# A pooling block, a gated recurrence and a 16,384-expert layer on one core: where 20 of the U tiles are transposed, and on which engine the low parts of one stage are made

## The chip, the cores and the metric

The kernel runs on one core of a Trainium2 chip. The metric is device time in microseconds (us): the median of three runs of the kernel before is 1994.73 us (1994.36 to 1997.6). A second time belongs to the one execution that was profiled, 1993.15 us, of which the profile's span covers 1991.4 us.

A core has five engines that run their own instruction streams in order: PE (matmul), DVE (vector), ACT (scalar), POOL (GpSimd) and SP, which here only issues DMA. They wait for each other through semaphores.

## The reference, cut to what matters

For 512 rows of 1024 columns, all in float32:

```
x = layer_norm(2**0.25 * x + pool_mixer(x), ln_g, ln_b)             # first block
ada = silu(c) @ w_ada + b_ada                                       # 6 shifts, scales, gates
z = modulate(rmsnorm(x)) @ w_in                                     # 5 sections of 512 columns
y_a = gate_b * causal_conv(gate_c * xa)
y_b = rg_lru(causal_conv(xr) + b) * gelu(gr)                        # a scan along the rows
x = x + g1 * (concat(head_rmsnorm(y_a), head_rmsnorm(y_b)) @ w_out)
h = modulate(rmsnorm(x))
q = h @ w_q; keys -> top 16 of 128, twice, 8 heads -> top 16 of 256 -> idx, g
x = x + g2 * sum_k g_k * gelu(U[idx_k] . h) * V[idx_k]              # U, V: 16384 x 1024
out = rmsnorm(x)
```

## The kernel before

Every large product is made from two halves of each float32 operand: a high part, rounded on ACT (`hi`), and a low part, the difference `src - hi` (`lo`). `mm3` (lines 139 to 141) then issues three matmuls: hi with hi, and two cross products. `split` makes both parts; its flag `pool` says whether the subtraction of the low part is on GpSimd (line 115) or on DVE (line 117). `wload` brings 512 KB of weights with one DMA (line 124) and splits them; it sends the low part to GpSimd when the count of loads is a multiple of `nload[1]`. That number is set stage by stage: 3 in the first block, `NZ` from the start of the product with `w_in`, none from the product with `w_q`, 2 from the dense expert part on. With `NZ = 1` all 31 weight tiles of `w_in` (20), `w_out` (8) and the first three heads of `w_q` have their low parts on GpSimd.

The stages, by the time in the profile:

- Up to about 353 us: the pooling block (line 339 to 343 also make the `ada` product on DVE beside it).
- 353 to 585 us, called the later front below: layer norm, `norm_T` (transposes of the rows by PE, line 461), the sections of `w_in` (`zchunk`, one chunk is 24 matmuls of 512 columns), two convolutions (lines 608 to 612), the recurrence `lru` (lines 635 to 660) and a head norm for each chunk (`headnorm`, lines 616 to 626, with a plain float32 matmul at line 620), then `w_out` (lines 737, 738) and the second norm.
- 585 to 955 us, called the middle: for 3 of the 4 row tiles the 16,384 experts are done densely. `q` and the key scores on PE, `top16` and `topk` on DVE (lines 856 to 860, 1012 to 1056), and from 743 us `g_tile`: DVE (1095, 1133) and ACT (1098, 1099) make one-hot tiles, PE multiplies them (1135), ACT copies the result out of PSUM (1136), and a DMA writes it to `g_d`. Beside this `stage_a` runs ahead: for tile `i` of 128 experts it computes gelu(U_i h) for 384 rows, 24 matmuls of 384 columns. `RT = 38` of the 128 tiles are done in the middle, 14 of them and 4 more ahead of `g_tile` in the program, the others spread through it by `run_a`.
- 955 to 1932 us, the main loop: for every tile of 128 experts `stage_v` multiplies gelu(U_i h) with the coefficients and V. The other 90 tiles of U are turned there by DVE. For the first row tile DVE and GpSimd gather rows of U and V instead (1181, 1193, 1204).

`stage_a` needs U_i with its columns on the partitions. In the middle there are two ways. Tiles `i < NU = 20` take way 4: `pre_u` has loaded them in the later front (160 DMAs of 64 KB, line 535, into `praw`), DVE has turned them in two halves each (`u_turn`, line 540, 40 instructions), and 40 DMAs have written them to the DRAM tensor `ut_d` (line 552); the middle loads them back (line 891) and splits them, ACT line 894 and DVE line 895, one instruction each of 1024 columns. The other 18 tiles take way 1 (`ATY`): the tile is loaded as it stands (line 878), PE transposes it in 8 pieces against an identity matrix into two of four PSUM side banks (line 882), and ACT (line 884) and DVE (line 886) make the high and low part from PSUM in two halves of 512 columns each.

`pre_u` is called once ahead of each of the 16 last chunks of `w_in` and turns one tile each time (`PU`), then the rest. The order on each engine is not the order of the code: a scheduler sets it from its own estimate of times, and the engines then keep to it. The lists under "The change" are of the built programs.

Of the kernel before, what the change touches and what calls it, by code (L numbers as in the profile page):

```python
# [33 lines left out]
AE = 5  # L34
T2 = ((0, 4), (4, 12))
AF_ = (1, 1, 0, 0)
NZ = 1
PRE = (('gn_b_2', 1), ('gn_b_2', 2))
TURN = {2: [('go', 1)], 3: [('lru', 0), ('conv', 0)], 6: [('lru', 1), ('go', 2)], 10: [('conv', 1), ('lru', 2), ('go', 3)], 
        13: [('lru', 3)], 14: [('conv', 2)]}  # L40
# [4 lines left out]
GP0 = 4  # L45
GL = 1
GE = 117
NU = 20
PU = (1,)
CB = 13  # L50
PL = 0
# [28 lines left out]
def _body(tc, nc, a, outer):  # L80
# [447 lines left out]
    U, W = a["expert_u_2"][0], a["expert_v_2"][0]  # L528
    ut_d = tc.dram_tile([max(1, NU), P, 2, KD * 64], F32, name="ut_d")
    npre = 0  # L530
# [11 lines left out]
    def pre_u(n):  # L542

        nonlocal npre
        for _ in range(n):
            if npre < NU:
                for h in range(2):
                    raw = up.tile([P, 2, 256], F32, name="praw", tag="praw")
                    u_load(raw, npre, 2 * h, 2)
                    ut = up.tile([P, KD, 64], F32, name="put", tag="put")  # L550
                    u_turn(ut, raw)
                    nc.sync.dma_start(ut_d[npre, :, h], ut.rearrange("p k e -> p (k e)"))
                npre += 1
# [35 lines left out]
    def zstart(sec, c):  # L589
        return wcols(a["w_in_2"][0], sec * 512 + c * P, P), bank()  # L590
# [83 lines left out]

    nload[1] = NZ
    zs = [zstart(*o) for o in ((3, 0), (4, 0), (3, 1), (4, 1))[:ZN]]
# [41 lines left out]

    pre_u(NU)

# [149 lines left out]
    def stage_a(i):  # L870
        uh = dn.tile([P, KD, P], F32R, name="uh", tag="uh", bufs=UB)
        ul = dn.tile([P, KD, P], F32R, name="ul", tag="ul", bufs=UB)
        ty = 4 if i < NU else ATY if i < RT else 2
        if ty != 1:
# [421 lines left out]
```

## Time and profile before

| | before |
|---|---|
| median of 3 runs | 1994.73 us |
| the profiled execution | 1993.15 us |
| its span | 1991.4 us |
| PE busy over the span | 1800.5 us (90%) |
| DVE busy | 1783.6 us (90%) |
| ACT busy | 830.8 us (42%) |
| POOL busy | 727.5 us (37%) |

PE and DVE are both busy for nine tenths of the span, so shares over the whole run say little about one stage. A stage is read from four views: the windows (what each engine does in a stretch, with the granted TensorE clock as a share of full speed), the groups of instructions (count, busy time, mean of one), the waits (who held whom), and the chain of waits, which is followed back from the last instruction of a stretch. Matmuls overlap each other: the step from one start to the next is what one costs, and the printed duration is longer.

### The profile page before, as it was taken

What the parts mean: (1) busy time and instruction counts of PE and PEld (TensorE: products, weight loads), DVE (VectorE), ACT (ScalarE), POOL (GpSimd) and SP (SyncE); (2) the same over time, 40 slices, a digit from 0 to 9 for tenths busy, and PEclk for the clock granted to TensorE, in tenths of its full rate; (3) what the DMA queues carried; (4) which work ended last, traced back from release to release, by engine and by line L of the source; (5) the groups of instructions that cost most, each with busy time, mean ns of one, the idle gap of its engine ahead of it and who ended that gap; (6) DMA issues with size and microseconds to landing.
All of it is one profiled execution on the core that took longest, in us unless ns stands there. A gap on an engine that the chain in (4) does not pass through costs nothing.

```text
span 1991.4 us, 26565 instructions
## 1 busy us (share of the span) xinstructions
PE 1800.5 (90%) x9003; PEld 1568.3 (79%) x9003; DVE 1783.6 (90%) x3088; ACT 830.8 (42%) x1318; POOL 727.5 (37%) x492
## 2 busy tenths in 40 slices
PE   8999889896899978888887999998999998989997
PEld 6787677765689978888766898888888887878886
DVE  8989888889868999996897998999999999999956
ACT  4433333444553339988332332333232333332334
POOL 3113222333351000000133655556565556565514
PEclk9999999998899989999998999999999999999999
DMA  5554574465554233545959999999999999999922
GB/s 163 180 166 128 190 250 131 140 203 179 172 159 135 76 112 139 202 179 205 294 199 281 299 285 292 302 296 309 306 298 296 310 299 289 305 293 306 293 102 96
DMA packets 288293, 441.13 MB, mean 222 GB/s; under 512 B 24600, under 2 KB 203652, under 8 KB 285084
## 3 DMA queue, kind: packets, MB, share of 16 engines
q1 hardware_dynamic: 251292, 305.19, 51.1%
q0 software_dynamic: 36864, 134.23, 20.5%
q8 instruction: 71, 1.16, 0.2%
q14 instruction: 66, 0.54, 0.1%
HBM read 393.11 MB, written 46.23 MB: 221 GB/s over the span
## 4 chain that ended last, share of the span: by engine, by line
DVE 36%; DMA 24%; PE 17%; issue 12%; ACT 7%; SPq 2%; POOL 2%; DVEq 0%; POOLq 0%; ACTq 0%
DMA uraw<-in_expert_u 11%; DVE ut L540 5%; DMA gu<-in_expert_u,idx 3%; DMA gv<-in_expert_v,idx 3%; DMA araw<-in_w_ada 3%; PE bank L139 3%; PE bank L141 3%; PE bank L140 3%; ACT gs L1136 2%; DVE acc L1204 2%; DVE ul L117 2%; DVE wlo L117 2%; ACT o L1098 2%; DVE junk L1193 2%; DVE sw L240 2%
## 5 line engine op out<-in xcount | busy, mean ns | idle before, releaser
L115 POOL TENSOR_TENSOR wlo<-wraw,whi 128x1024 fp32r<-128x1024 f32 x111 | 292.3, 2635 | 782.4 <-ACT whi L113 766.8
L141 PE MATMUL aux<-h2h,ul 128*128 128x384 f32 x1024 | 360.7, 353 | 59.8 <-DVE ul L117 53.5
L139 PE MATMUL aux<-h2h,uh 128*128 128x384 f32 x1024 | 355.9, 348 | 4.9 <-ACT uh L884 1.8
L140 PE MATMUL aux<-h2l,uh 128*128 128x384 f32 x1024 | 353.6, 345 | 0.0
L113 ACT ACTIVATE whi<-wraw 128x1024 fp32r<-128x1024 f32 x218 | 228.3, 1051 | 196.4 <-DMA wraw<-in_expert_v 68.5
L140 PE MATMUL o<-wlo,wh 128*128 128x512 f32 x756 | 297.7, 394 | 13.8 <-DVE wlo L117 13.7
L141 PE MATMUL o<-whi,wl 128*128 128x512 f32 x756 | 296.6, 392 | 0.0
L139 PE MATMUL o<-whi,wh 128*128 128x512 f32 x756 | 290.1, 395 | 5.2 <-ACT whi L113 5.2
L141 PEld LDWEIGHTS aux<-h2h,ul 128*128 128x128 f32 x1024 | 198.6, 194 | 76.6 <-DVE ul L117 68.7
L1181 POOL DMA_INDIRECT gv<-in_expert_v,idx x128 | 186.8, 1460 | 186.0 <-DVE acc L1204 150.4
L1181 POOL DMA_INDIRECT gu<-in_expert_u,idx x128 | 167.5, 1309 | 161.3 <-DVE junk L1193 127.7
L139 PEld LDWEIGHTS aux<-h2h,uh 128*128 128x128 f32 x1024 | 198.6, 194 | 10.3 <-ACT gl L905 2.4
L113 ACT ACTIVATE uh<-ut 128x1024 fp32r<-128x1024 f32 x90 | 95.3, 1058 | 262.2 <-PE aux L140 174.5
L540 DVE STREAM_TRANSPOSE ut<-uraw 128x1024 f32<-128x1024 f32 x90 | 200.0, 2222 | 4.7 <-DMA uraw<-in_expert_u 4.7
L140 PEld LDWEIGHTS aux<-h2l,uh 128*128 128x128 f32 x1024 | 197.9, 193 | 3.7
L1193 DVE SCALAR_TENSOR_TENSOR junk<-gu,hrow 128x1024 bf16<-128x1024 f32 x128 | 168.3, 1315 | 19.8 <-DMA gu<-in_expert_u,idx 19.6
L1204 DVE SCALAR_TENSOR_TENSOR acc<-gv,cf,acc 128x1024 f32<-128x1024 f32 x127 | 169.6, 1335 | 17.6 <-DMA gv<-in_expert_v,idx 15.1
L140 PEld LDWEIGHTS o<-wlo,wh 128*128 128x128 f32 x756 | 143.3, 190 | 43.9 <-DVE wlo L117 16.5
L113 ACT ACTIVATE wh<-gl 128x384 fp32r<-128x384 f32 x128 | 66.7, 523 | 253.2 <-PE o L140 234.3
L139 PEld LDWEIGHTS o<-whi,wh 128*128 128x128 f32 x756 | 143.3, 190 | 33.0 <-ACT whi L113 6.1
L141 PEld LDWEIGHTS o<-whi,wl 128*128 128x128 f32 x756 | 143.3, 189 | 30.7
L117 DVE TENSOR_TENSOR wlo<-wraw,whi 128x1024 fp32r<-128x1024 f32 x107 | 150.6, 1409 | 7.2 <-ACT whi L113 7.2
(376 smaller groups left out, 3607.4 us busy)
## 6 DMA issues: line engine op xcount, KB each, us to landing
wraw<-in_expert_v SPq DMA_DIRECT2D x128, 512.0 KB
uraw<-in_expert_u SPq DMA_DIRECT2D x360, 128.0 KB
araw<-in_w_ada SPq DMA_DIRECT2D x96, 256.0 KB
g_d<-gs SPq DMA_DIRECT2D x24, 1024.0 KB
gt<-g_d SPq DMA_DIRECT2D x15, 1536.0 KB
wraw<-in_pool_w_in SPq DMA_DIRECT2D x32, 512.0 KB
wraw<-in_w_in SPq DMA_DIRECT2D x20, 512.0 KB
praw<-in_expert_u SPq DMA_DIRECT2D x160, 64.0 KB
```

Source lines behind the costliest of these rows:

```text
L113: S.activation(hi, src, AF.Copy)
L115: G.tensor_tensor(lo, src, hi.bitcast(F32), op=OP.subtract)
L117: V.tensor_tensor(lo, src, hi.bitcast(F32), op=OP.subtract)
L139: i = PE.matmul(out, lhsT=l[0], rhs=r[0], start=first, stop=False)
L140: PE.matmul(out, lhsT=l[0], rhs=r[1], start=False, stop=False)
L141: PE.matmul(out, lhsT=l[1], rhs=r[0], start=False, stop=last)
L240: V.tensor_tensor(nxt[:, :, step:], cur[:, :, step:], cur[:, :, :T - step], op=OP.add)
L540: V.transpose(out=ut.rearrange("p k (a r) -> p a k r", r=32), in_=raw.rearrange("p a (c k) -> p a k c", k=KD))
L1098: S.activation(o2[:, u], iorow, AF.Abs, bias=sT[:, 1, t0 + u:t0 + u + 1], scale=-1.0)
L1181: G.indirect_dma_start(out=r, out_offset=None, in_=src, in_offset=bass.IndirectOffsetOnAxis(ap=idx[t][:, s:s + 1], axis=0))
L1193: paced(V.scalar_tensor_tensor(junk, r, 1.0, hrow[t], op0=OP.mult, op1=OP.mult, accum_out=cf[t][:, s:s + 1]))
L1204: paced(V.scalar_tensor_tensor(acc[t], r, cf[t][:, s:s + 1], acc[t], op0=OP.mult, op1=OP.add))
```

## The change

Two numbers change. With `NU = 0` nothing is turned ahead: `pre_u` does nothing, `ut_d` is not used, and `stage_a` takes way 1 for all 38 tiles. With `NZ = 1 << 30` no count is a multiple, so the 31 low parts of the later front are made by DVE.

```diff
 AF_ = (1, 1, 0, 0)
-NZ = 1
+NZ = 1 << 30
 PRE = (('gn_b_2', 1), ('gn_b_2', 2))
...
 GE = 117
-NU = 20
+NU = 0
 PU = (1,)
```

Instructions in the two built programs, by engine:

| engine | instruction | before | after |
|---|---|---|---|
| SP | DMA `praw<-in_expert_u` (L535) | 160 | 0 |
| SP | DMA `ut_d<-put` (L552) | 40 | 0 |
| SP | DMA `ut<-ut_d` (L891) | 20 | 0 |
| SP | DMA `uraw<-in_expert_u` (L878) | 18 | 38 |
| DVE | STREAM_TRANSPOSE `put<-praw` (L540) | 40 | 0 |
| DVE | `wlo<-wraw,whi` (L117) | 107 | 138 |
| POOL | `wlo<-wraw,whi` (L115) | 111 | 80 |
| PE | MATMUL `aux<-ident,uraw` (L882) | 144 | 304 |
| ACT | `uh<-ut` (L894), 1024 columns | 20 | 0 |
| ACT | `uh<-aux` (L884), 512 columns | 36 | 76 |
| DVE | `ul<-ut,uh` (L895), 1024 columns | 20 | 0 |
| DVE | `ul<-aux,uh` (L886), 512 columns | 36 | 76 |

DVE in the later front, inside the second `lru` (lines 654 to 660; `xr` is the next convolution). Before:

```order
L655 TENSOR_TENSOR s__3710<-s__3710,w__3711 128x512
L656 SCALAR_TENSOR_TENSOR r<-r,w__3711 128x512
L540 STREAM_TRANSPOSE put<-praw 128x2x8x32
L658 TENSOR_TENSOR s__3710<-s__3710,i 128x512
L540 STREAM_TRANSPOSE put<-praw 128x2x8x32
L659 SCALAR_TENSOR_TENSOR i<-r,s__3710 128x512
L660 TENSOR_TENSOR i<-i,ge 128x512
L610 TENSOR_SCALAR xr<-zr,cols 128x512
L612 SCALAR_TENSOR_TENSOR xr<-zr,cols,xr 128x511
L540 STREAM_TRANSPOSE put<-praw 128x2x8x32
L612 SCALAR_TENSOR_TENSOR xr<-zr,cols,xr 128x510
```

The same place on DVE after the change:

```order
L117 TENSOR_TENSOR wlo<-wraw,whi 128x1024
L655 TENSOR_TENSOR s__3662<-s__3662,w__3663 128x512
L656 SCALAR_TENSOR_TENSOR r<-r,w__3663 128x512
L658 TENSOR_TENSOR s__3662<-s__3662,i 128x512
L659 SCALAR_TENSOR_TENSOR i<-r,s__3662 128x512
L660 TENSOR_TENSOR i<-i,ge 128x512
L117 TENSOR_TENSOR wlo<-wraw,whi 128x1024
L610 TENSOR_SCALAR xr<-zr,cols 128x512
L612 SCALAR_TENSOR_TENSOR xr<-zr,cols,xr 128x511
```

The transposes are gone from between the steps of the recurrence, and low parts of weights stand there instead, fewer of them.

DVE in the middle, in the search for the top 16 of the first heads (`sc` are scores, `top` and `ti` values and places, `pos` and `pb` the places among the candidates). Before, one low part of a whole U tile:

```order
L1025 MAX_INDEX pos<-best,tmpk 128x8
L1051 TENSOR_TENSOR g<-best 128x48
L1033 CAST pb<-pos 128x48
L895 TENSOR_TENSOR ul<-ut,uh 128x2x8x64
L1042 TENSOR_TENSOR cmp__5617<-pb,offt 128x768
L1043 TENSOR_TENSOR prod<-cmp__5617,dt 128x768
L1044 TENSOR_REDUCE i_5335<-prod 128x48
L856 MAX top_5274<-sc 128x8 x2
```

The same place after the change:

```order
L886 TENSOR_TENSOR ul<-aux,uh 128x512
L1023 MAX best<-tmpk 128x8
L1025 MAX_INDEX pos<-best,tmpk 128x8
L1051 TENSOR_TENSOR g<-best 128x48
L1033 CAST pb<-pos 128x48
L1042 TENSOR_TENSOR cmp__5309<-pb,offt 128x768
L886 TENSOR_TENSOR ul<-aux,uh 128x512
L1043 TENSOR_TENSOR prod<-cmp__5309,dt 128x768
L856 MAX top_4954<-sc 128x8 x2
```

Halves of low parts, read from PSUM, stand where one whole low part stood. Ahead of the first top-16 instruction DVE has 5 whole low parts before and 5 halves after; ahead of its first `og` (L1133) it has all 20 whole ones before and 36 halves after.

PE in the middle, just ahead of the first matmul of `g_tile` (L1112 transposes the chosen indices and weights, L1135 is the product of one-hot tiles). Before:

```order
L1112 MATMUL aux<-ident,g 128x128
L139 MATMUL aux<-h2h,uh 128x384
L140 MATMUL aux<-h2l,uh 128x384
L141 MATMUL aux<-h2h,ul 128x384
L882 MATMUL aux<-ident,uraw 128x128 x8
L1135 MATMUL bank<-og,o_6753 128x128 x8
```

The place of the same three transposes of indices and weights (L1112) after the change:

```order
L1112 MATMUL aux<-ident,i_5015 128x128
L139 MATMUL aux<-h2h,uh 128x384
L140 MATMUL aux<-h2l,uh 128x384
L1112 MATMUL aux<-ident,i_5016 128x128
L1112 MATMUL aux<-ident,g 128x128
L882 MATMUL aux<-ident,uraw 128x128 x4
L141 MATMUL aux<-h2h,ul 128x384
```

Before, the first tile turned by PE stands right ahead of the first L1135, and 480 matmuls of 384 columns (20 tiles) stand in front of it. After, transposes stand between the matmuls from the first tile on: 160 of them (20 tiles) and 444 matmuls of 384 columns (18.5 tiles) are ahead of the first L1135. Ahead of the last matmul of key scores there are 233 matmuls of 384 columns before, and after the change 168 with 63 transposes.

## Rows read from the trace of the kernel before

**Rows 1.** Windows by stage: busy us (instructions) per engine; PEclk, DMA share.

```profile
353.00:402.00 49.00, 40.05 (x262) 36.46 (x261) 43.55 (x70) 23.68 (x51) 18.49 (x17) 0.93 0.48 146
402.00:540.00 138.00, 110.56 (x407) 80.72 (x406) 123.04 (x130) 69.60 (x90) 45.28 (x18) 0.89 0.61 191
585.00:720.00 135.00, 132.78 (x794) 126.13 (x794) 124.95 (x568) 53.88 (x84) 12.13 (x8) 1.00 0.43 136
720.00:757.00 37.00, 21.00 (x107) 20.46 (x106) 37.00 (x199) 19.50 (x42) 0.00 (x0) 0.72 0.10 38
757.00:955.00 198.00, 176.46 (x1283) 170.34 (x1282) 169.44 (x496) 182.16 (x341) 0.70 (x1) 1.00 0.53 195
```

**Rows 2.** Groups, 353 to 585 us: count, busy us, mean ns, idle before.

```profile
L540 DVE STREAM_TRANSPOSE put<-praw 128x512 f32<-128x512 f32 x40 | 46.2, 1158 | 12.8 <-DMA praw<-in_expert_u 12.7
L115 POOL TENSOR_TENSOR wlo<-wraw,whi 128x1024 fp32r<-128x1024 f32 x29 | 72.3, 2495 | 129.6 <-ACT whi L113 117.7 <-DMA praw<-in_expert_u 11.9
L612 DVE SCALAR_TENSOR_TENSOR cx<-gc,cols,cx 128x511 f32<-128x511 f32 x4 | 9.2, 2301 | 0.1
L612 DVE SCALAR_TENSOR_TENSOR xr<-zr,cols,xr 128x511 f32<-128x511 f32 x4 | 3.0, 746 | 0.1
```

**Rows 3.** Waits, 353 to 585 us: total, times, longest.

```profile
PE aux L620 <- ACT sq L616: 27.4, 5, 9.1
DVE put L540 <- DMA praw<-in_expert_u: 12.7, 6, 4.0
```

**Rows 4.** Chain of waits, 353 to 585 us: shares by line.

```profile
by line: DVE put L540 13.9%; issue 12.5%; DMA praw<-in_expert_u 10.1%; SPq L535 6.8%; PE bank L139 6.7%; PE bank L140 6.5%; PE bank L141 6.4%; DVE xr L612 2.9%; DVE cx L612 2.8%; DVE q L653 2.7%; DVE r L656 1.7%; SPq L552 1.6%; PE aux L620 
```

**Rows 5.** Timeline, GpSimd and then DVE, at 421 us: start, duration.

```profile
421.20 2.48 POOL L115 TENSOR_TENSOR wlo<-wraw,whi 128x1024 fp32r<-128x1024 f32 x1 [3.69 <-ACT whi L113]
421.36 2.88 DVE L656 SCALAR_TENSOR_TENSOR r<-r,w__3530 128x512 f32<-128x512 f32 x1
```

**Rows 6.** DVE, line 117, whole run: ns min/median/max; first, last start.

```profile
L117 DVE TENSOR_TENSOR wlo<-wraw,whi x107: 1202/1216/4129, 10.5 to 1956.4; 128x1024 fp32r<-128x1024 f32 x107
```

**Rows 7.** Groups on PE, 402 to 540 us: the plain fp32 matmuls.

```profile
L620 PE MATMUL aux<-sq,blk 128*128 128x512 f32 x13 | 11.7, 1010 | 27.4 <-ACT sq L616 27.4
L636 PE MATMUL aux<-xr,wri 128*128 128x512 f32 x8 | 4.1, 592 | 0.0
```

**Rows 8.** Timeline of PE at full clock: start, duration.

```profile
559.72 0.39 PE L140 MATMUL bank<-wlo,y 128*128 128x512 f32 x1
559.95 0.39 PE L141 MATMUL bank<-whi,y 128*128 128x512 f32 x1
...
574.92 1.05 PE L461 MATMUL aux<-ident,xn 128*128 128x128 f32 x8
...
649.36 0.34 PE L139 MATMUL aux<-h2h,uh 128*128 128x384 f32 x1
649.53 0.34 PE L140 MATMUL aux<-h2l,uh 128*128 128x384 f32 x1
```

**Rows 9.** Chain of waits again: one head norm on PE, start and us.

```profile
547.45 0.86 PE aux L620 x2
```

**Rows 10.** Groups, 585 to 757 us: low part of a tile turned ahead.

```profile
L895 DVE TENSOR_TENSOR ul<-ut,uh 128x1024 fp32r<-128x1024 f32 x20 | 24.3, 1214 | 3.2 <-ACT uh L894 3.2
```

**Rows 11.** Groups, 757 to 955 us: the pieces of a tile turned by PE.

```profile
L886 DVE TENSOR_TENSOR ul<-aux,uh 128x512 fp32r<-128x512 f32 x33 | 22.1, 681 | 17.6 <-ACT uh L884 17.6
L884 ACT ACTIVATE uh<-aux 128x512 fp32r<-128x512 f32 x33 | 19.8, 612 | 5.1 <-PE aux L882 5.1
L882 PE MATMUL aux<-ident,uraw 128*128 128x128 f32 x136 | 20.4, 276 | 2.9 <-ACT gl L905 2.9
```

**Rows 12.** Waits of PE, 585 to 757 us.

```profile
PE aux L1112 <- DVE i L1044: 9.2, 1, 9.2
PE bank L1135 <- ACT o L1099: 6.8, 1, 6.8
```

**Rows 13.** Chain of waits, 757 to 955 us: shares by line.

```profile
by line: ACT gs L1136 24.4%; ACT o L1098 20.8%; ACT o L1099 8.6%; issue 8.3%; PE bank L1135 7.5%; ACT uh L884 4.7%; DVE og L1133 3.4%; PE aux L141 3.1%; PE aux L139 3.1%; PE aux L140 2.8%; ACT gl L905 2.4%; DMA g_d<-gs 1.9%; DMA gt<-g_d 1.7
```

## Prediction

> **What bounds the kernel now.** I read the windows first, because PE and DVE are both at 90% over the whole run and only a stage shows which of them ends last. In the later front PE is the one that waits: in 402 to 540 us it is busy 110.6 of 138 us at a granted clock of 0.89, and DVE is busy 123.0 [rows 1]. At 585 to 720 us both are nearly full (PE 132.8, DVE 125.0 of 135), at 720 to 757 us DVE is full and PE idles 16 us, and at 757 to 955 us ACT is the fullest, 182 of 198 us [rows 1].
>
> Next the groups, the waits and the chain of the later front. The 40 transposes ahead of time take DVE 46.2 us there [rows 2]. PE's main wait is for the head norms, 27.4 us in 5 waits, and DVE itself waits 12.7 us for the pieces of U that it is to turn [rows 3]. The chain of waits says the same in another way: of its 232 us, 13.9% are these transposes, 10.1% the DMAs into `praw` and 6.8% their issue on SP, together 71 us [rows 4]. The work ahead of time is not hidden here; it is a large part of what ends last.
>
> A second cost is in the low parts on GpSimd. The same vector operation of 511 columns takes 2301 ns in one group of four and 746 ns in another [rows 2]. The timeline shows where the difference comes from: at 421.20 us GpSimd starts a low part of 2.48 us, and the DVE operation that starts at 421.36 lasts 2.88 us, about as long as the GpSimd one [rows 5]. So a low part on GpSimd can hold one DVE operation for about 2.1 us.
>
> **The change, part by part.**
>
> *Later front, DVE.* Busy in 353 to 540 us: 43.6 + 123.0 = 166.6 us [rows 1]. Taken away: 46.2 us of transposes [rows 2]. Taken away too: the holding by GpSimd. From below, the one group of four at 2301 ns gives 4 x 1.55 = 6 us; from above, each of the 29 low parts holds something for 2.1 us, 61 us. I take 25 us, somewhat under half, since only some low parts find DVE at such an operation. Added: 29 low parts at 1.216 us [rows 6], 35.3 us at most. DVE then has 166.6 - 46.2 - 25 + 35.3 = 130.7 us to do.
>
> *Later front, PE.* In 402 to 540 us it issues 407 matmuls [rows 1]. Of these 13 + 8 + 8 are plain float32 (line 635 has as many as 636) [rows 7], at 0.43 us each by the 0.86 us for two [rows 9], 12.5 us. The other 378 have 512 columns and step by 0.23 us at full clock [rows 8], 86.9 us. PE needs 99.4 us of the 138, so 38.6 us are waits and slow clock. In 353 to 402 us it is idle for another 9 us [rows 1]. At most 47.6 us can go; PE then needs 139 us in which DVE has 131. As DVE is still that full and works in a chain with ACT (recurrence, then head norm), the two won't fit without gaps. If PE's 27.4 us of waits for the head norms all stayed, 20 us would go; if all went, 48. I take 31, two thirds of the most, as about 71 us of the present chain vanish and at most 35 us come back.
>
> *Queues.* SP loses 160 + 40 issues in the later front, among which the weight loads stood; nothing is moved behind a longer wait there. In the middle 20 loads of `uraw` stand where 20 loads of `ut` stood.
>
> *Middle, ahead of the first L1135.* PE gets 152 more transposes and, by the built order, 36 fewer matmuls of 384 columns. Eight transposes took 1.05 us in the front [rows 8], 0.13 us each, so +19.9 us; the matmuls step by 0.17 us, so -6.1 us: +13.8 us on PE. From above, at the printed 276 ns each [rows 11], it is +42 - 6 = +36 us. Against this stand the 16 us that PE idles in 720 to 757 us, made up of its waits for the indices, 9.2 us, and for the one-hot tiles, 6.8 us [rows 12]; beside these it runs at a clock of 0.72 there [rows 1]. DVE ends this stretch, since it is the one that is full. Between its first top-16 instruction and its first `og` it has 31 halves at 681 ns [rows 11] in place of 15 whole low parts at 1214 ns [rows 10]: 21.1 - 18.2 = +2.9 us. But the first scores stand 36 matmuls earlier and 16 transposes later, -6.1 + 2.1 = -4.0 us. So DVE's end moves by -1 us if PE and ACT deliver in time, and by up to 36 - 16 = +20 if each transpose costs what is printed. I take +2, close to DVE's sum, as the gap in front of the indices is as wide as the work that PE gets.
>
> *Middle, from the first L1135.* The 36 matmuls and 8 transposes come back here: 6.1 + 1.0 = 7.1 us of PE; ACT gets 4 more halves at 612 ns, 2.4 us, DVE 4 at 681 ns, 2.7 us [rows 11]. The chain here is mostly ACT (lines 1136, 1098 and 1099 are 54%) with some PE [rows 13], so the price lies between 2.4 and 7.1; I take 5.
>
> At this place a rule of the Trainium skill speaks against the change. In 757 to 955 us 136 transposes by PE keep it busy for 20.4 us, 0.15 us each [rows 11], and the granted clock of that window is 1.00 [rows 1]. The page "TensorE: Matmul & The Clock Gate" (Part 4: PE-mode transpose) says that one took about 275 ns in a kernel and that transposes do not raise the clock as other matmuls do. By that figure the 160 transposes would be 44 us, an estimate from that page, and the sum 24 us worse, near no change; the trace has the same number as a printed duration but not as a step, so I keep 0.13.
>
> *Main loop.* Its instructions stay; its start on the DMA queues shifts. I take 0 (-4 to +4).
>
> **Sum.** -31 + 2 + 5 + 0 = -24 us on the profiled execution's 1993.15 us: 1969 us. The median of the runs is 1.6 us above that execution, so I forecast 1970 us. With the ends of the terms (-48 to -20; -1 to +20; +2.4 to +7.1; -4 to +4) the forecast's own range is 1955 to 1985.
>
> **Rivals.**
>
> *PE takes back all it lost.* With the transposes, the DMA waits and the holding gone, DVE has slack and PE runs through: -48 - 1 + 2 = -47, 1948 us. For it: DVE's 131 us are below PE's 139. Against: the chain between ACT and DVE inside each recurrence remains.
>
> *The middle takes it all.* The gap at 720 to 757 us is of no use, because each transposed tile needs ACT and then a DVE that is full before PE can go on, and each of the four side banks is held meanwhile. Then PE's +19.9 us all count, with 5 us after and about 5 us of waits: -31 + 30 = -1, 1994 us. For it: DVE is full there. Against: only the third product of a tile needs the low part, and the program puts the transposes of the next tile in front of it.
>
> *The low part's wait moves to DVE.* This one is slower. GpSimd now waits 117.7 us in front of its low parts for the high parts from ACT [rows 2], and nothing but the other low parts stands behind it. On DVE the same wait would hold the recurrence, the head norms and so PE. If a third of it, 39 us, meets a DVE that has other work, the front is 8 us slower, the middle 7 us: +15, 2010 us. It decides from 24 us on, a fifth of that wait. For it: DVE runs in order, and the loads that ACT waits for come through the same queue. Against: the scheduler puts the low part among other DVE work at the time when it expects the high part.
>
> *The clock falls in the middle.* If runs of transposes let it fall in 585 to 757 us as it does now in 402 to 540 us, to 0.89 [rows 1], 11% of 172 us is 19 us, of which PE's gap hides a few: 1985 us. It is the other half of the skill's rule; the 1.00 at 757 to 955 us speaks against it.
>
> *It doesn't do what it says.* The built program shows that all 38 tiles go through PE and 31 low parts move, so I give this nothing.
>
> **Chances and range.** Forecast 0.56, PE takes back all 0.12, the middle takes it all 0.10, the wait on DVE 0.17, the clock 0.05. No change means within 0.2%, 4 us, about what a measurement of this kernel can tell. Forecast, first rival, clock and a fifth of the second count as faster: 0.56 + 0.12 + 0.05 + 0.02 = 0.75; the third rival and 0.01 of the second are slower, 0.18; 0.07 of the second is the same. The range of 8 in 10 goes from 1945, just beyond the first rival, to 2000, which leaves out most of the third.
>
> **What would show it.** Right: the group of 511 columns at 2301 ns falls to about 750; PE's waits for the head norms fall below 12 us; the clock of the later front rises above 0.95; `w_out` and the second norm end near 554 us in place of 585; the middle lasts within 10 us of today's 370; PE's wait for the indices shrinks below 5 us. Wrong: new waits of DVE for ACT's high parts of more than 20 us in the later front; a middle over 385 us; a granted clock below 0.95 in 585 to 720 us; or a main loop that differs by more than 5 us from 1036 us, which nothing in this sum foresees.

## The result, and the profile after

The changed kernel takes 1963.42 us in the median of 4 runs (1957.91 to 1967.59); its ratio to the kernel before is 0.984, 95% interval 0.981 to 0.987. A second series of it gave 1955.43 us, ratio 0.981 (0.978 to 0.983). It is faster, by 31 us in the first series and, by the ratio, 39 in the second, where 24 were forecast. Its profiled executions took 1957.91 and 1951.71 us, against 1993.15 us and, for a second profile of the kernel before, 1997.54 us.

To compare stages that begin at different times I cut each trace at the same events: the first layer norm of the rows (line 501), the weight load of the first gate matmul (635), the first product that takes up a `w_out` result (737), the first copy of key scores (844), the first `og` (1133), the first and the last product `gl*gt` of the main loop (932). Lengths in us:

| from, to | before | before, again | after | after, again |
|---|---|---|---|---|
| start, layer norm | 336.2 | 337.3 | 338.9 | 337.3 |
| layer norm, gates | 65.9 | 67.4 | 64.9 | 64.8 |
| gates, `w_out` | 156.5 | 157.1 | 119.5 | 119.6 |
| `w_out`, scores | 60.4 | 60.4 | 57.8 | 61.2 |
| scores, first `og` | 126.1 | 127.0 | 128.0 | 128.0 |
| first `og`, main loop | 209.5 | 210.2 | 218.3 | 219.5 |
| main loop | 977.1 | 976.6 | 968.7 | 959.5 |
| rest | 59.7 | 59.8 | 60.0 | 60.0 |

"The front" below is the second and third row together: 222.3 us before, 184.4 after. The windows of the kernel before at these marks, as in [rows 1]. The columns are the stretch, its length, the busy us (instructions) of PE, of PE's weight loads, of DVE, ACT and GpSimd, then the granted clock, the DMA share and GB/s:

```profile
336.20:402.10 65.90, 54.55 (x345) 48.69 (x344) 59.93 (x100) 30.08 (x64) 25.82 (x25) 0.95 0.41 124
402.10:558.60 156.50, 129.06 (x487) 95.55 (x486) 134.81 (x144) 78.09 (x102) 52.90 (x21) 0.90 0.58 182
619.00:745.10 126.10, 113.23 (x621) 106.24 (x620) 125.76 (x694) 41.30 (x67) 0.00 (x0) 0.96 0.27 91
745.10:954.60 209.50, 182.67 (x1311) 176.56 (x1312) 180.95 (x536) 193.92 (x367) 0.30 (x1) 0.98 0.50 186
```

The same four of the changed kernel, and its main loop:

```profile
338.90:403.80 64.90, 53.32 (x347) 48.26 (x346) 53.50 (x103) 31.38 (x66) 5.96 (x17) 0.92 0.27 76
403.80:523.30 119.50, 119.50 (x490) 91.87 (x488) 93.67 (x130) 76.35 (x100) 0.00 (x0) 1.00 0.31 92
581.10:709.10 128.00, 123.80 (x725) 116.83 (x724) 127.16 (x710) 43.45 (x80) 0.00 (x0) 0.99 0.29 93
709.10:927.40 218.30, 195.21 (x1389) 191.19 (x1387) 183.47 (x541) 198.29 (x377) 0.87 (x1) 0.96 0.52 186
927.40:1896.10 968.70, 897.10 (x4278) 794.71 (x4277) 911.84 (x1122) 308.09 (x431) 509.04 (x316) 0.97 0.96 288
```

From the gates to `w_out` PE is now busy for every one of the 119.5 us, at a granted clock of 1.00 instead of 0.90; DVE is busy for 93.7 us where it was for 134.8. Of the 37.0 us that went, 27.4 are PE's waits for the head norms; the other 9.6 are busy time (129.1 against 119.5 us for about as many matmuls, 487 and 490 in the traces), at the lower granted clock. The groups of the front answer [rows 2 and 6]:

```profile
L117 DVE TENSOR_TENSOR wlo<-wraw,whi 128x1024 fp32r<-128x1024 f32 x30 | 36.6, 1220 | 15.5 <-ACT whi L113 15.5
L612 DVE SCALAR_TENSOR_TENSOR xr<-zr,cols,xr 128x511 f32<-128x511 f32 x4 | 3.0, 750 | 0.1
L612 DVE SCALAR_TENSOR_TENSOR cx<-gc,cols,cx 128x511 f32<-128x511 f32 x4 | 3.0, 744 | 0.0
```

The operation that took 2301 ns takes 744, and the low parts cost DVE 36.6 us and 15.5 us of waiting for ACT. All of PE's waits of the front, against [rows 3]:

```profile
PE aux L461 <- DVE rq L438: 8.0, 1, 8.0
PE aux L461 <- DVE xn L448: 2.9, 1, 2.9
PE bank L139 <- ACT ah L113: 0.6, 1, 0.6
```

The wait for the head norms (27.4 us) is gone. The chain of the front, against [rows 4], is now PE's three products, 63%, in place of transposes and their DMAs:

```profile
by line: PE bank L139 21.1%; PE bank L140 20.9%; PE bank L141 20.9%; DVE wlo L117 3.9%; issue 3.6%; PE aux L620 3.3%; DMA wraw<-in_w_in 2.3%; DMA wraw<-in_w_q 2.2%; PE aux L636 1.9%; PE aux L635 1.9%; DVE st L498 1.7%; ACT nf L469 1.6%; DVE
```

The instruction of [rows 5] that lasted 2.88 us beside GpSimd, in the timeline after (start, duration):

```profile
416.92 0.69 DVE L656 SCALAR_TENSOR_TENSOR r<-r,w__3530 128x512 f32<-128x512 f32 x1
```

In the middle, all of PE's waits from `w_out` to the first `og` [rows 12]:

```profile
PE aux L141 <- DVE ul L886: 3.7, 4, 2.0
PE aux L139 <- ACT uh L884: 0.8, 1, 0.8
PE bank L139 <- DVE ot L737: 0.6, 1, 0.6
PE aux L882 <- ACT gl L905: 0.5, 2, 0.3
```

The wait for the indices, 9.2 us, has vanished: the transposes fill it. From the first `og` to the main loop the groups of [rows 11] are:

```profile
L886 DVE TENSOR_TENSOR ul<-aux,uh 128x512 fp32r<-128x512 f32 x38 | 25.8, 685 | 12.2 <-ACT uh L884 12.2
L882 PE MATMUL aux<-ident,uraw 128*128 128x128 f32 x156 | 24.9, 282 | 11.2 <-ACT gl L905 11.2
L884 ACT ACTIVATE uh<-aux 128x512 fp32r<-128x512 f32 x39 | 23.1, 612 | 4.9 <-PE aux L882 3.4 <-DVE o L1095 1.5
```

PE's transposes now wait 11.2 us for ACT's gelu (line 905), 2.9 before, but all of PE's idle time in this stretch fell, from 26.8 to 23.1 us. Its busy time rose by 12.5 us: counted in the traces, it has 458 matmuls of 384 columns there in place of 401, and 154 transposes in place of 136.

### The profile page after: what moved, and what is told of

Same layout as the page of the kernel before. It is cut to its first block, busy times and chain, and to the rows that moved or that the text cites. A ratio compares the mean times of both kernels' runs of the same rounds, so it can differ in the third digit from the quotient of the medians.

```text
span 1956.1 us, 26521 instructions
## 1 busy us (share of the span) xinstructions
PE 1809.1 (92%) x9163; PEld 1587.4 (81%) x9163; DVE 1741.4 (89%) x3099; ACT 833.3 (43%) x1338; POOL 643.8 (33%) x461
## 4 chain that ended last, share of the span: by engine, by line
DVE 33%; PE 27%; DMA 24%; issue 8%; ACT 5%; POOL 2%; SPq 1%; DVEq 0%; POOLq 0%; ACTq 0%
DMA uraw<-in_expert_u 13%; DVE ut L540 4%; PE bank L141 4%; PE bank L140 4%; PE bank L139 4%; DMA gv<-in_expert_v,idx 3%; DMA gu<-in_expert_u,idx 3%; DVE wlo L117 2%; PE aux L141 2%; PE bank L1135 2%; PE aux L139 2%; PE aux L140 2%; DVE acc L1204 2%; DVE junk L1193 2%; DMA araw<-in_w_ada 2%
## 5 line engine op out<-in xcount | busy, mean ns | idle before, releaser
L115 POOL TENSOR_TENSOR wlo<-wraw,whi 128x1024 fp32r<-128x1024 f32 x80 | 210.9, 2637 | 642.7 <-ACT whi L113 640.8
L141 PEld LDWEIGHTS aux<-h2h,ul 128*128 128x128 f32 x1024 | 199.4, 195 | 79.5 <-DVE ul L117 66.5
L1181 POOL DMA_INDIRECT gv<-in_expert_v,idx x128 | 194.3, 1518 | 181.1 <-DVE acc L1204 153.4
L1181 POOL DMA_INDIRECT gu<-in_expert_u,idx x128 | 158.9, 1242 | 171.9 <-DVE junk L1193 119.2
L117 DVE TENSOR_TENSOR wlo<-wraw,whi 128x1024 fp32r<-128x1024 f32 x138 | 177.2, 1285 | 28.1 <-ACT whi L113 28.1
L540 DVE STREAM_TRANSPOSE ut<-uraw 128x1024 f32<-128x1024 f32 x90 | 199.5, 2218 | 2.4 <-DMA uraw<-in_expert_u 2.4
L1204 DVE SCALAR_TENSOR_TENSOR acc<-gv,cf,acc 128x1024 f32<-128x1024 f32 x127 | 174.5, 1374 | 17.4 <-DMA gv<-in_expert_v,idx 17.2
L1193 DVE SCALAR_TENSOR_TENSOR junk<-gu,hrow 128x1024 bf16<-128x1024 f32 x128 | 179.6, 1403 | 11.7 <-DMA gu<-in_expert_u,idx 11.4
## 6 DMA issues: line engine op xcount, KB each, us to landing
uraw<-in_expert_u SPq DMA_DIRECT2D x360, 128.0 KB
```

The lines of the kernel that those rows point to most:

```text
L115: G.tensor_tensor(lo, src, hi.bitcast(F32), op=OP.subtract)
L117: V.tensor_tensor(lo, src, hi.bitcast(F32), op=OP.subtract)
L141: PE.matmul(out, lhsT=l[1], rhs=r[0], start=False, stop=last)
L540: V.transpose(out=ut.rearrange("p k (a r) -> p a k r", r=32), in_=raw.rearrange("p a (c k) -> p a k c", k=KD))
L1181: G.indirect_dma_start(out=r, out_offset=None, in_=src, in_offset=bass.IndirectOffsetOnAxis(ap=idx[t][:, s:s + 1], axis=0))
L1193: paced(V.scalar_tensor_tensor(junk, r, 1.0, hrow[t], op0=OP.mult, op1=OP.mult, accum_out=cf[t][:, s:s + 1]))
```

## The experiments

Each kernel was timed in five rounds beside the kernel before; "ratio" is to it, with the 95% interval. First, which half of the edit made the front shorter. Theory A: DVE's transposes and their traffic held PE. Theory B: GpSimd's low parts did, by holding DVE's operations.

**The first edit alone**, on the kernel before:

```diff
-NU = 20
+NU = 0
```

> The kernel before with the first edit alone (`NU = 0`): nothing is turned ahead, the 31 low parts of the later front stay on GpSimd. The stretch meant is that from the first gate product (line 635) to the first `w_out` product (line 737), 156.5 us before and 119.5 after. Theory A (PE was held by the transposes ahead of time: DVE's own 46 us for them and the loads and stores that go with them): the stretch falls to 118-126 us and the time comes to 1960-1970 us, as after. Theory B (PE was held by GpSimd's low parts, which stretch DVE's operations by some 41 us in all): DVE keeps its long operations, the stretch only falls to 135-145 us and the time to 1975-1985 us.

Measured: 1969.32 us, ratio 0.987 (0.984 to 0.990). The two windows of the front (layer norm, then gates to `w_out`):

```profile
335.50:400.40 64.90, 53.54 (x335) 47.96 (x334) 53.95 (x90) 31.22 (x65) 26.29 (x25) 0.92 0.23 65
400.40:540.00 139.60, 123.42 (x486) 92.12 (x485) 108.40 (x113) 76.10 (x101) 52.92 (x21) 0.96 0.27 81
```

The stretch, 139.6 us, is B's, the time A's. It gets there by a main loop of 954.9 us, 22 us shorter than before, which neither theory spoke of (below); the stretches from `w_out` to the loop, 413.7 against 396.0 us, take 18 of these back. In the front the first edit alone is worth 18 of 38 us.

**The second edit alone:**

```diff
-NZ = 1
+NZ = 1 << 30
```

> The kernel before with the second edit alone (low parts of the later front on DVE): the 20 tiles are still turned ahead by DVE. Theory A: DVE has 46 us of transposes and 35 us of low parts in the later front, about 145 us of work in a stretch in which PE needs 119, so the stretch from line 635 to line 737 stays at 145-158 us and the time at 1985-2000 us. Theory B: no operation of DVE is stretched any more, the stretch falls to 125-135 us and the time to 1965-1975 us. In both the middle keeps its 370 us, so a front as short as that of the changed kernel would give about 1953-1957 us.

Measured: 1992.56 us, ratio 0.999 (0.996 to 1.001), no difference. The front:

```profile
337.40:411.10 73.70, 56.75 (x352) 50.98 (x351) 60.10 (x109) 30.79 (x65) 5.76 (x17) 0.86 0.45 131
411.10:560.50 149.40, 127.32 (x486) 95.14 (x484) 127.94 (x164) 77.86 (x101) 0.00 (x0) 0.91 0.59 183
```

The stretch is A's; with the layer norm 8 us longer, the front stays at 223.1 us. Alone, then, the two edits bring 18 and -1 us of front, together 38.

**GpSimd makes low parts a second time** in the later front of the changed kernel. The edit reaches the 20 weight tiles of `w_in`, not the 29 that the expectation speaks of:

```diff
+        if twice:
+            G.tensor_tensor(twice[0].tile([P, 1024], F32R, name="lo2", tag="lo2", bufs=1), raw, hi.bitcast(F32), op=OP.subtract)
```

> The changed kernel, in whose later front GpSimd makes each low part a second time into a tile that nothing reads; DVE's work and order stay as they are. Theory B (a GpSimd operation on two inputs holds an operation of DVE for about its own length): some 29 operations of 2.5 us on GpSimd, DVE's busy time in the stretch from line 635 to line 737 rises from 94 to 115-135 us, and the stretch from 119.5 to 130-145 us; the time comes to 1972-1988 us. Theory A (the holding matters little): DVE rises by less than 10 us, the stretch stays at 119-122 us, the time at 1958-1968 us.

Measured: 1987.55 us, ratio 0.997 (0.994 to 0.9995). The front:

```profile
334.80:411.20 76.40, 59.09 (x346) 52.83 (x344) 61.42 (x99) 30.78 (x65) 33.01 (x26) 0.84 0.21 59
411.20:554.30 143.10, 126.91 (x490) 95.42 (x490) 119.96 (x134) 77.51 (x101) 32.58 (x11) 0.93 0.27 79
```

As B expects, DVE's busy time rises from 93.7 to 120.0 us, and the stretch to 143.1. One form in it, held in one place and free in another (the lines of this kernel stand 3 lower in the file; its 658 is 655 elsewhere):

```profile
L658 DVE TENSOR_TENSOR s__3537<-s__3537,w__3538 128x512 f32<-128x512 f32 x1 | 2.8, 2849 | 0.0
...
L658 DVE TENSOR_TENSOR s__3887<-s__3887,w__3888 128x512 f32<-128x512 f32 x1 | 0.7, 695 | 0.0
```

The first ran beside a second low part on GpSimd, the second beside nothing there. The layer norm, 11.5 us longer, counts less: some of GpSimd's own steps of it now stand behind the second low parts.

**The transposes alone:** the changed kernel with 40 transposes by DVE of one resident tile:

```diff
+    still = up.tile([P, 2, 256], F32, name="still", tag="still", bufs=1)
+    u_load(still, 0, 0, 2)
...
-                    u_turn(ut, raw)
-                    nc.sync.dma_start(ut_d[npre, :, h], ut.rearrange("p k e -> p (k e)"))
+                    u_turn(ut, still)
```

> The changed kernel with 40 more transposes on DVE in the later front, all of one tile that is loaded once; nothing reads what they make, and the loads and stores of U stay away. Theory A1 (what the turning cost was DVE's own time): DVE's 94 us in the stretch from line 635 to line 737 become about 125, and as that stretch has so far lasted DVE's busy time and 21 to 31 us more, it grows from 119.5 to 140-152 us; the time comes to 1980-1995 us. Theory A2 (what it cost were the 200 DMAs and their issue on SP, 71 us of the chain of waits before together with the transposes): the stretch stays at 120-126 us and the time at 1955-1970 us.

Measured: 1985.44 us, ratio 0.995 (0.992 to 0.998). The front:

```profile
337.30:424.60 87.30, 63.25 (x374) 56.22 (x372) 83.29 (x134) 32.06 (x66) 6.04 (x17) 0.86 0.21 61
424.60:553.40 128.80, 118.39 (x462) 88.81 (x462) 104.77 (x140) 76.96 (x100) 0.00 (x0) 0.96 0.28 84
```

A1 has the time, and the front (216.1 us) is longer by what it expects, but not in the place that it names: the stretch, 128.8 us, is in neither theory's band. With no loads to wait for, the scheduler wrote many transposes early; in the chain twelve stand in a row (start, us):

```profile
397.62 11.69 DVE put L540 x12
```

**The traffic alone:** the changed kernel with the 160 loads of U and 40 stores, and no transposes:

```diff
-                    ut = up.tile([P, KD, 64], F32, name="put", tag="put")
-                    u_turn(ut, raw)
-                    nc.sync.dma_start(ut_d[npre, :, h], ut.rearrange("p k e -> p (k e)"))
+                    nc.sync.dma_start(ut_d[npre, :, h], raw.rearrange("p a d -> p (a d)"))
```

> The changed kernel with the 160 loads of U and the 40 stores to DRAM of before in the later front, the stores straight from the loaded tiles; no transposes, and nothing reads the stores. Theory A1: the stretch from line 635 to line 737 stays at 119-124 us, the time at 1955-1968 us. Theory A2: weights arrive later behind these DMAs and their issue, the stretch grows to 130-150 us, and the time comes to 1970-1990 us.

Measured: 1978.86 us, ratio 0.992 (0.989 to 0.995). From the gates to `w_out`:

```profile
404.30:556.20 151.90, 127.92 (x490) 95.26 (x488) 98.19 (x134) 78.37 (x102) 0.00 (x0) 0.91 0.65 195
```

The stretch is 2 us beyond A2's band and the time is A2's, with DVE hardly busier than after. The waits of the whole front, 340 to 556 us, name the reason, DVE's and then ACT's (us, times, longest):

```profile
DVE wlo L117 <- ACT whi L113: 46.8, 15, 8.8
```

```profile
ACT whi L113 <- DMA wraw<-in_w_in: 29.9, 8, 10.7
ACT whi L113 <- DMA wraw<-in_w_out: 15.8, 3, 11.7
```

The weights land late, ACT's high parts are late, and DVE, in order, stands in front of the low parts. This is the prediction's third rival, the wait that moves to DVE, at 46.8 us; it did not come with the change, which takes the traffic away at the same time, nor with the second edit alone (11.9 us in its front), where DVE is itself late. SP, which issues all these DMAs in order, stands in front of the loads and stores of U itself (the store, line 552 elsewhere, is line 550 in this kernel):

```profile
SPq L535 <- DMA ut_d<-praw: 31.7, 38, 2.8
SPq L550 <- DMA praw<-in_expert_u: 16.2, 33, 1.7
```

In the front of the kernel before, it stood in front of the stores for DVE's transposes:

```profile
SPq L552 <- DVE put L540: 42.9, 30, 4.6
```

So this kernel holds the queue in another way than the kernel before does, and its 31 us are not exactly the traffic's share there. No run took the bytes and the held queue apart; the DMA share of the stretch, 0.65 against 0.96 in the main loop, speaks for the queue.

**The middle spared:** the changed kernel with the middle of the kernel before (untransposed tiles are loaded, as the expectation says):

```diff
-NU = 0
+NU = 20
...
-            if npre < NU:
+            if npre < 0:
...
-            nc.sync.dma_start(ut.rearrange("p k e -> p (k e)"), ut_d[i].rearrange("p h d -> p (h d)"))
+            nc.sync.dma_start(ut.rearrange("p k e -> p (k e)"), U[i * P:(i + 1) * P, :])
```

> The changed kernel, whose first 20 U tiles are loaded in the middle with the load and the split of the kernel before, but without having been transposed (the result is that of untransposed tiles): the later front is that of the changed kernel, the middle that of the kernel before. From `w_out` to the main loop the changed kernel took 404 to 409 us, the kernel before 396. If the transposes on PE are the price of the middle, this kernel has 393-398 us there and ends 6-12 us below the changed kernel, at 1945-1956 us. If the middle is longer for another reason (an earlier start, another state of the DMA queues), it keeps 403-410 us and 1955-1966 us.

Measured: 1948.04 us, ratio 0.975 (0.971 to 0.979), and 392.1 us from `w_out` to the main loop, just below the band of the first guess: 12 to 17 us less than the changed kernel, 4 to 6 less than the kernel before. That the turning by PE costs this much is not shown, though. From `w_out` to the first `og` the two kernels take the same 185.8 us, where PE has 12 transposes here and 150 in the changed kernel. The difference lies behind it, where this kernel has 402 matmuls of 384 columns and 132 transposes against 458 and 154; and `NU = 3` below, with 35 of the 38 tiles turned by PE, takes 396.3 us from `w_out` to the loop, as long as the kernel before.

**The changed kernel again, and the kernel before again,** both without an edit:

> The changed kernel once more, unchanged, for the size of what a second execution shows: the main loop (from the first to the last product of line 932) took 968.7 us in it and 977.1 us in the kernel before, the middle from the first L1135 to the main loop 218.3 against 209.5. If the 8.4 us of the main loop belong to the change, this execution has 966-971 us; if they are scatter between executions, 972-980 us or a second profile of the kernel before would come as low. Time expected by both: 1958-1968 us.

> The kernel before once more, unchanged. In its first profile the main loop took 977.1 us, in those of the changed kernel 968.7 and 959.5. If this difference is scatter between executions, this one has 958-972 us or the runs spread over it; if it belongs to the kernel, 974-980 us. The front is expected to repeat within 3 us (stretch from line 635 to 737: 154-159 us), the time is 1986-2004 us by both.

Measured: 1955.43 us and 1995.08 us (ratio 0.999, 0.997 to 1.002). The fronts repeat within 2.2 us. The main loops are 959.5 us (968.7 in the first profile, so one kernel can differ by 9) and 976.6 us (977.1). For the kernel before the loop is its own, then; for the changed kernel neither guess held.

What goes with the main loop is the order in which the scheduler wrote it. In the traces the last 900 instructions on DVE stand in one of four orders; within an order they are the same, whatever was edited. That gave a test, since three tiles turned ahead bring back the order of before, and two or four do not:

```diff
-NU = 0
+NU = 2
```

and 3 and 4 in the same place.

> The changed kernel with two tiles turned ahead (`NU = 2`). The scheduler then writes the rest of the program in the order that it has in the kernel with the first edit alone and in the one with the traffic alone, whose main loops took 954.9 and 956.9 us; the changed kernel's order took 968.7 and 959.5, that of the kernel before 977.1 and 976.6 (and 978.6 with another front and middle). Theory O (the length of the main loop belongs to the order that the scheduler wrote, and to little else): main loop 952-960 us, front from layer norm to `w_out` 184-188 us, time 1943-1955 us. Theory S (the main loop scatters from execution to execution): 955-977 us, and 1950-1965 us.

> The changed kernel with three tiles turned ahead (`NU = 3`): one tile more than in the kernel with two, but in the main loop the scheduler's order is that of the kernel before. Theory O: main loop 974-980 us, 18-25 us longer than with two or four tiles, time 1955-1970 us. Theory S: main loop within 8 us of theirs, 1945-1960 us.

> The changed kernel with four tiles turned ahead (`NU = 4`); its main loop stands in the same order as with two tiles. Theory O: main loop 952-960 us, front 184-191 us (8 transposes, 9 us of DVE, of which the slack of 26 us beside PE hides most), time 1943-1957 us. Theory S: main loop 955-977 us, as with three tiles, 1950-1965 us.

Measured, for 2, 3 and 4 tiles: 1961.02 us (ratio 0.984, 0.980 to 0.989), 1966.28 (0.987, 0.982 to 0.991), 1957.68 (0.983, 0.979 to 0.987). The main loops are 966.0, 971.6 and 955.0 us; only the last is inside theory O's band, and two of the three times are theory S's. But the premise for two tiles was wrong: that kernel's last 900 DVE instructions differ in 232 places from those of the kernels that it was to match, an order of its own. All profiles by order, in us, the stretch from the first `og` to the main loop beside it:

| order | kernel | first `og` to loop | main loop | sum |
|---|---|---|---|---|
| 1 | before | 209.5 | 977.1 | 1186.6 |
| 1 | before, again | 210.2 | 976.6 | 1186.8 |
| 1 | middle spared | 206.3 | 978.6 | 1184.9 |
| 1 | `NU = 3` | 209.3 | 971.6 | 1180.9 |
| 1 | `NU = 12` | 208.2 | 983.3 | 1191.5 |
| 2 | after | 218.3 | 968.7 | 1187.0 |
| 2 | after, again | 219.5 | 959.5 | 1179.0 |
| 2 | low parts on DVE | 210.7 | 966.1 | 1176.8 |
| 2 | GpSimd too | 218.4 | 970.5 | 1188.9 |
| 2 | transposes alone | 215.0 | 970.7 | 1185.7 |
| 3 | nothing turned ahead | 220.9 | 954.9 | 1175.8 |
| 3 | traffic alone | 223.7 | 956.9 | 1180.6 |
| 3 | `NU = 4` | 220.6 | 955.0 | 1175.6 |
| 4 | `NU = 2` | 221.6 | 966.0 | 1187.6 |

The loops of the first three orders don't overlap: means of 977, 967 and 956 us. But the stretch in front of the loop is mostly longer where the loop is shorter. One reason can be counted: in order 3 PE has 912 matmuls of 384 columns between `w_out` and the loop, in the others 881 to 890, about one tile (24 matmuls) less, 4 us at the step of 0.17 us. The sums of orders 1 and 2, means of 1186 and 1184, lie inside each other's scatter of 5 to 7 us either way; those of order 3, mean 1177, lie below all of order 1. The 8 us that the changed kernel (order 2) loses ahead of the loop and the 8 to 17 it gains in it are thus mainly one amount on two sides of a mark. What else in the order does it is open.

**Twelve tiles turned ahead:**

```diff
-NU = 0
+NU = 12
```

> The changed kernel with twelve tiles turned ahead (`NU = 12`); main loop in the order of the kernel before (974-980 us by theory O). The front, from layer norm to `w_out`, took 184 us with none and 223 us with twenty, and 216 us with the turning or the traffic of twenty alone. If the cost grows evenly with the tiles, it is 184 + 12 x 2 = 208 us here; if DVE's 26 us of slack and the gaps on SP take the first half for nothing, 184-195 us. Time: 1975-1988 us by the first, 1953-1970 us by the second.

Measured: 1980.81 us, ratio 0.994 (0.991 to 0.996); front 211.1 us; main loop 983.3 us, in the order of the kernel before but above theory O's band. There is no free first half: with the low parts on DVE, 2, 3 and 4 tiles turned ahead cost 6.7, 9.3 and 10.1 us of front, 12 cost 26.7 and 20 cost 38.7. The expectations for 2 and 4 tiles, fronts of at most 188 and 191 us, both failed (191.1 and 194.5). The fronts together, DVE's busy time from the two windows of each:

| kernel | front, us | DVE busy, us | front over 184.4, per us of DVE over 147.2 |
|---|---|---|---|
| after | 184.4 | 147.2 | |
| `NU = 2` | 191.1 | 151.4 | 1.6 |
| `NU = 3` | 193.7 | 153.4 | 1.5 |
| `NU = 4` | 194.5 | 155.3 | 1.2 |
| nothing turned ahead, low parts on GpSimd | 204.5 | 162.3 | 1.3 |
| `NU = 12` | 211.1 | 171.8 | 1.1 |
| GpSimd too | 219.5 | 181.4 | 1.0 |
| low parts on DVE, 20 turned | 223.1 | 188.0 | 0.9 |
| transposes alone | 216.1 | 188.1 | 0.8 |
| before | 222.3 | 194.7 | 0.8 |
| traffic alone | 215.8 | 147.7 | not by DVE |

In the three kernels that have no traffic of U (nothing turned ahead, GpSimd too, transposes alone) a microsecond on DVE costs 0.8 to 1.3 of front, whether it is a transpose or an operation held by GpSimd, though DVE is busy for only 79 to 87% of it. The others have the traffic as well, and cost 0.8 to 1.6; for 2 to 4 tiles all but 1 us of it lies in the layer norm stretch. The way to PE is the same in the five kernels that carry only some of the costs: its waits for the head norms, none in the changed kernel, are 9.7 us with the first edit alone, 21.2 with the second, 16.1 with GpSimd too, 9.5 with the transposes and 22.3 with the traffic alone. The traffic costs 31 us without DVE's busy time, and beside a DVE already late it shows little: 20 turned ahead with transposes and traffic (223.1) is 7 us above the transposes alone.

The spared middle aside, which leaves work out, none of these kernels is shown to beat the changed one: `NU = 4` is at 0.983 (0.979 to 0.987), the changed kernel at 0.984 and 0.981.

## Why the prediction was right, and where its terms were off

*Bounds.* The reading of the front held: PE waited there for a chain of DVE work and DMA. Rows 2 to 5 named the three costs, and each, put back alone, returned most of the gain.

*Later front, DVE.* Forecast 166.6 to 130.7 us, -36 (353 to 540 us); measured by marks 194.7 to 147.2, -47.5. The transposes (-46.2) and low parts (+36.6 against 35.3) were right. The mis-sized term is the holding by GpSimd, "25 us, somewhat under half": for every DVE instruction that overlaps GpSimd I took its duration less the shortest of the same line and shape, and the sum is 43.7 us before and 0.6 after. At 2.1 us each, some 20 of the 29 low parts held something, not 12. The page "SBUF — State Buffer" of the Trainium skill (section "SBUF: two separate sides") describes it: a DVE instruction with two inputs in SBUF and a GpSimd one that reads SBUF exclude each other, and the loser waits for the whole instruction. The trace agrees: in the kernel with the second low parts one form takes 2849 ns beside GpSimd and 695 without. The three terms as measured come to -53; the 5 us between this and -47.5 were not traced.

*Later front, PE.* Forecast -31, "two thirds of the most"; measured -37.9, and -40.1 between the second profiles. The reason I gave for keeping a third, that PE and DVE, in a chain with ACT, "won't fit without gaps", failed from the gates to `w_out`: PE was busy 119.5 of 119.5 us. In this stretch the first rival was right. For the whole kernel its 1948 us was too low: PE's idle time in the layer norm, of which I had counted 9 us among what can go, stayed (11.4 us before, 11.6 after).

*Queues.* I gave the SP issues and DMAs no price of their own beside the chain's share; put back alone they cost 31 us.

*Middle ahead of the first L1135.* Forecast +2 (-1 to +20). From `w_out` to the first matmul of line 1135, at 750.4, 754.4, 719.2 and 721.1 us in the four profiles, it is 191.8 and 192.7 us before, 195.9 and 199.4 after: +4.1 and +6.7. The second rival, the middle takes it all, was wrong: of its 30 us 4 to 7 came here, as PE's gap took most of the transposes.

*Middle from the first L1135.* Forecast +5 (2.4 to 7.1); measured 204.2 and 205.0 us before, 208.2 and 209.3 after, +4.0 and +4.3, inside. (From the first `og`, the mark of the tables, it is +8.8 and +9.3: 12 matmuls more lie behind that mark, and 9 came out of the main loop.) The price of 24 us more by the page "TensorE: Matmul & The Clock Gate" of the Trainium skill (Part 4: PE-mode transpose), which the prediction weighed, did not come true here: the middle is 8 to 11 us longer in all. The granted clock is 0.99 and 0.96 in the two windows with 128 and 156 transposes, but these stand among many other matmuls (725 and 1389 in all), so no run here tests the page's rule for transposes alone.

*Main loop.* Forecast 0; measured -8.4 and -17.1. The prediction's own test (more than 5 us) fired. The work is all but the same, its order is not; with the stretch from the first `og` on, the change is +0.4 and -7.8. What in the order does it stays open.

*Third rival and clock.* DVE waits 15.5 us for high parts, below the 20 that would have spoken for it; the mechanism is real and showed under traffic. The clock of the middle held.

*Range.* The ends of the terms add up to 1944 to 2006 us, not to the 1955 to 1985 that I wrote beside them; the measured time lies in either.

The forecast was thus right in sign and cause, and some 7 us short in the time of the first series (1963.42 against 1970), 15 in the second. By the profiled executions the change is -35 and -46 us where -24 was forecast: 7 to 9 us more than forecast went in the front, and 8 to 17 in the main loop, which the sum had at 0; some of it came back elsewhere. What is left open: by the runs the spared middle is worth 7 to 15 us to the end, while its profile (1952.4 us of span against 1956.1 and 1949.9) shows nothing of it; that profile is the slowest of its six runs, the first one of the changed kernel the fastest of its four.

## What to carry to other kernels

An engine at 80% in a stage can still be its bound: where it stands in a chain with others, as DVE does here, expect a microsecond added to it to cost about one of time, holding included, and don't take its idle share for slack. Put costs back one at a time as well as taking them away: here one edit alone gave half the gain of the front and the other none, since the costs hid each other. Measure a forecast's terms at the marks that it named: another mark moved 5 us from one term to the next. Where a scheduler writes the order, a change in one stage re-orders the next, so compare sums across a mark before a gain or loss is called that stage's.

## What the runs showed that was not expected

GpSimd's 11 second low parts between the gates and `w_out`, 32.6 us, lengthened the DVE instructions that they overlap by 22.6 us (each against the shortest of its line and shape): two thirds of GpSimd's busy time came back as DVE's. And an edit in the front alone (low parts on DVE) changed the order of a main loop 400 us later, which took 966.1 us in place of 977.1.
